# Pairs of seven products for retention's gates and second value blocks and for the last blocks of the attention's output projection, in a 256-token hybrid decoder layer on one Trainium2 core

## The chip, the cores and the metric

The kernel runs on one core of one Trainium2 chip, as one program. The core has a matrix engine (TensorE, "PE" in the profile), two engines for elementwise work that are used here (VectorE, "DVE", and ScalarE, "ACT"), GpSimd ("POOL"), and SyncE ("SP"), which mostly issues transfers. The metric is the device time of one execution in microseconds (us); lower is better. Where several executions are timed, their median is given.

## The reference

The layer takes `x` of 256 tokens by 2048 features (float32), a memory of 256 by 2048, and the weights of one decoder layer. What it computes, cut to what matters:

```python
hn = rmsnorm(x, w_mix)
z = hn @ w_in            # 2048 x 14336: q, k (1024 each), v, gate (2048 each), xr, yr, ga, gb (2048 each)
ret  = head_groupnorm(chunkwise_retention(rotary(q), rotary(k), v)) * silu(gate)   # 8 heads
rnn  = gelu(yr) * rg_lru(causal_dwconv(xr))
m    = sigmoid(ga) * (ret @ w_proj_ret) + sigmoid(gb) * (rnn @ w_proj_rnn)
h1   = x + m @ w_mix_out
h2   = h1 + cross_attention(rmsnorm(h1), rmsnorm(mem)) @ xa_w_o     # 4 heads of 512
out  = rmsnorm(h2 + (silu(gate') * val') @ ffn_w_down)              # gate', val' from a conv of rmsnorm(h2) @ ffn_w_up
```

Nearly all of the arithmetic is the product of a 256 x 2048 operand with a weight matrix. The transfers of weights total some 370 MB.

## The kernel before, in words

**Blocks and units.** Every weight matrix is cut into blocks of 512 columns (`BW`), and a block into units of 512 rows: a unit is one weight tile `raw` of 128 partitions by 4 x 512 numbers (1 MB). The list of all blocks in the order in which they are computed is written out by hand (`weight_plan`), and the transfers of the weights follow it, on SyncE's queue, into five buffers.

**Products in three parts.** Float32 accuracy is made of three products of a faster format. Each `raw` is split into `hi` (a cast on ACT, L281) and `lo = raw - hi` (on DVE, L282); each operand tile likewise. A 512-column product of 128 rows by 128 tokens is then the three products hi·hi, lo·hi and hi·lo. In `gemm_n` (token-major result) the lines are L357, L358 and L364, in `gemm_t` (feature-major result) L346. A plain block of `gemm_n` has four units of 24 products each, 96 in all.

**Pairs of seven products.** For some pairs of neighbouring blocks the kernel uses `pair_products`: half of the shared dimension of the two blocks is multiplied by a scheme of Strassen's kind with seven products instead of eight, and the other half plainly. `PAIR_UNITS` lists its eleven units in order: q1, p, q3, p, p, q5, q2, q6, p, q7, q4. The seven q's have 12 products each and the four p's ("plain") 24, 180 in all. The q's need sums of weight tiles. Two of these are made by transfers that add to what is in the buffer, issued by GpSimd (L262), and two by additions of whole tiles on DVE (L287 and L289). They also need sums of the operand's tiles, which `sums` makes (L498 to L504) and the caller passes as `ss`. The results are three accumulators, `xz`, `yu` and `rw`, and after each unit `out(kind, ...)` moves finished parts: `pair_out` into two new tiles in memory (copies L451, additions L457, subtractions L467), `pair_add` into rows that exist already (L424). There are three accumulators in all (pool `pm`), shared by pairs and plain blocks.

**What sets the order of the work around.** While one unit is multiplied, `prefetch` prepares the splits of the units after it, up to two ahead; there are three buffers each for `hi` and `lo`. Smaller work (scores and values of a retention head, its normalisation, transposes, the recurrence) is put between units by hand: `later(n, fn)` runs `fn` when n+1 further units have ended, whatever the length of these units. Within each engine, the order of instructions is fixed when the program is built, by a scheduler that works on data dependences and on the order in which the code records them; each engine then works through its own list and waits for others through semaphores.

**Retention.** Two groups g of four heads. For each, the plan has q, half of v, k, the other half of v and two blocks of gates. `retain` puts the scores of head hh after unit hh+1 that follows, the values (L515) one unit later, and after the fourth head `normalise`: statistics of DVE (L784, L785), a power on GpSimd (L607), the subtraction and gating (L797) and the scaling on ACT (L802). The transposes of heads 1 and 2 on PE (`finish_head`, L527) come two units after that, those of heads 3 and 4 three units. For the first group all this lies in the second group's q and first v block. `rotated` (L713 to L719) turns q and k on DVE.

**The operand's sums.** `x`'s scaled tiles `xs` are split once and kept. The sums of x that pairs need (`xs_sums`, four tiles) are made by `sum_x`, called inside the second and third blocks of the recurrent branch; their first reader is the pair of gates `O_GA` after it.

**Residuals.** `residual` computes mix_out and xa_w_o: blocks 0 and 1 as a pair by `pair_add`, blocks 2 and 3 plainly. After each block it takes the squares of the new rows (L1037 is such a square) and transposes them (`turn`, splits L571 and L572) into the next stage's operand, again by `later`. After xa_w_o comes ffn_up, whose k-th unit reads the transposed blocks in order. The two last stages, ffn_up and ffn_down, run in three parts; two of them use pairs for ffn_down.

The change touches `weight_plan`, `residual_plan`, the call of `out` in `pair_products`, `pair_add`, the loop over g with its gates, the place of `sum_x`, and `residual`.

Of the kernel before, what the change touches and what calls it, by code (L numbers as in the profile page):

```python
# [63 lines left out]
def weight_plan():  # L64

    w0 = "w_in"
    plan = []
    for g in range(2):
        for c in (O_Q, O_K):
            plan += [(w0, 0, NT, c + g * BW), (w0, 0, NT, O_V + g * 1024 + (c == O_K) * BW)]  # L70
        plan += [(w0, 0, NT, O_G + g * 1024 + b * BW) for b in range(2)]
    for b in range(4):
# [22 lines left out]
def residual_plan(w):  # L95
    return [(w, 0, NT, 0, BW)] + [(w, 0, NT, b * BW) for b in (2, 3)]

# [52 lines left out]
def hybrid_layer(  # L150
# [229 lines left out]
    def pair_products(w, row, st, ss, c0, c1, out):  # L380
# [18 lines left out]
        for kind, parts in units(*e):  # L399
# [18 lines left out]
            with tc.high_priority(URGENT):  # L418
                out(kind, x, z, yu, rw)

    def pair_add(w, row, st, ss, c0, c1, h0, h1):

        def add(o, i, op=ALU.add):
            dve.tensor_tensor(out=o, in0=o, in1=i, op=op)  # L424

        def out(kind, x, z, yu, rw):
            if kind == "q1":
                add(h0[:, 0, :], x)
            elif kind == "q5":
                later(2, lambda: add(h1, rw))  # L430
                later(3, lambda: add(h1, z[:, None, :].to_broadcast([P, 2, BW])))
            elif kind == "q6":
                add(h1[:, 0, :], x, ALU.subtract)
            elif kind == "q7":
                add(h0[:, 1, :], x)
                add(h1[:, 1, :], x, ALU.subtract)
            elif kind == "q4":
                add(h0, yu)

        pair_products(w, row, st, ss, c0, c1, out)  # L440
# [312 lines left out]
    def retain(g, qr, kr, vs, dec, gates):  # L753
# [51 lines left out]
        for hh in range(4):  # L805
            later(hh, lambda hh=hh: scores(hh))

    for g in range(2):
        dec = big([P, 4, S], s="dec")
        vs, turned = [], []  # L810
        for b, o in enumerate((O_Q, O_K)):
# [6 lines left out]
            if g > 0:  # L818
                turned.append(rotated(a))
            v = gemm_n("w_in", 0, xs, NT, O_V + g * 1024 + b * BW)  # L820
            if g == 0:
                turned.append(rotated(a))
            vs.append(split_rows(v, rs0))
        qr, kr = turned
        gates = []
        for b in range(2):
            a = gemm_n("w_in", 0, xs, NT, O_G + g * 1024 + b * BW)
            t = big([P, 2, BW], s="gate")
            for tt in range(2):
                act.activation(t[:, tt, :], a[:, tt, :], AF.Tanh, scale=half_rs0[:, tt : tt + 1])  # L830
            dve.scalar_tensor_tensor(out=t, in0=t, scalar=1.0, in1=a, op0=ALU.add, op1=ALU.mult)
            gates.append(t)
        retain(g, qr, kr, vs, dec, gates)
# [105 lines left out]

    xs_sums = []  # L940

    def sum_x(i):

        t = tmp("xt")
        sp.dma_start(out=t, in_=x_t[:, 2 * i : 2 * i + 2, :])
        for j in range(2):
            act.activation(t[:, j, :], t[:, j, :], AF.Identity, scale=p_mix(2 * i + j))
        xs_sums.append(sums(t))

    merged, merged_sums = [], []  # L950
# [11 lines left out]
    for b in range(4):  # L962
        if b in (1, 2):
            for i in range(2):
                later(2 + 4 * i, lambda i=2 * b - 2 + i: sum_x(i))
        recurrent(b)
# [36 lines left out]
    def residual(w, st, ssum, out, osum, wcol, steps=None):  # L1003

        ss = sp_.tile([P, 2, 4], F32, tag="ss0", name=nm("ss"))
        for bs in ((0, 1), (2,), (3,)):
            if steps:
                steps(bs[0])
            if len(bs) > 1:
                pair_add(w, 0, st, ssum, 0, BW, hrow[0], hrow[1])  # L1010
            else:
                h = hrow[bs[0]]
                dve.tensor_add(h, h, gemm_n(w, 0, st, NT, bs[0] * BW))
            for i, b in enumerate(bs):
                squares(hrow[b], ss, b)
                for pr in range(2):
                    later(2 * i + pr, lambda b=b, pr=pr: turn(b, pr, out, osum, wcol))
        return ss
# [286 lines left out]
```

## Time and profile before

| | |
|---|---|
| device time, median of 3 runs | 2017.65 us (2015.16 to 2017.88) |
| the profiled execution | 2014.64 us, of which the span of the trace is 2012.9 us |
| PE (TensorE) busy | 1999.0 us, 99% of the span, 10120 products |
| DVE (VectorE) busy | 1528.7 us, 76% |
| ACT (ScalarE) busy | 1131.6 us, 56% |
| POOL (GpSimd) busy | 36.0 us, 2% |
| transfers | 426.77 MB, 212 GB/s on average |
| granted clock of PE | 0.999 of full speed on average |

The profile is of one execution. A group line names a line of the kernel, the engine, the operation, what is written and read, and how often; then the busy time in us and the mean of one in ns, and behind the last bar the idle time of that engine just before, with what ended most of it. A line of the timeline gives the start and the duration in us, and in square brackets the idle time before it. Products on PE overlap: the next starts before the record of the last ends, so the time that one costs is read from the distance of the starts.

### The profile page before, as it was taken

The page shows a single profiled execution, that of the slowest core. Times are in us where ns is not written, and L with a number is a line of the kernel's source. Part 1 is how long each engine was busy: PE and PEld are TensorE (multiplying, and loading weights), DVE is VectorE, ACT ScalarE, POOL GpSimd, SP SyncE. Part 2 cuts the span into 40 slices and gives each one's busy share as a digit, 9 for nine tenths or more (in the row PEclk, how much of TensorE's full clock was granted, in tenths as well). Part 3 has the DMA queues.
Part 4 walks back from the last instruction along what each step waited for, and adds up shares of the span by engine and source line. Part 5 has one row for each costly group of instructions (what it writes and reads, how often), then busy time and mean ns, then how long its engine had stood idle before and what let it go on. Part 6 is the DMA issues. An engine that isn't in the chain of part 4 may idle for free.

```text
span 2012.9 us, 24896 instructions
## 1 busy us (share of the span) xinstructions
PE 1999.0 (99%) x10120; PEld 1702.0 (85%) x10120; DVE 1528.7 (76%) x1551; ACT 1131.6 (56%) x1143; POOL 36.0 (2%) x44
## 2 busy tenths in 40 slices
PE   9999999999999999999999999999999999999998
PEld 8888888888888888888888888888878888888887
DVE  6747657889985887778888767587797787886775
ACT  6445446777765554566666655455554555544552
POOL 0000000000000000000000000000000000000000
PEclk9999999999999999999999999999999999999999
DMA  9554555655887765777886746454567555675552
GB/s 369 217 205 160 209 199 184 218 195 165 246 270 260 224 235 188 229 277 221 262 270 205 249 147 230 169 198 179 187 209 232 202 186 196 187 232 187 202 196 84
DMA packets 75426, 426.77 MB, mean 212 GB/s; under 512 B 8240, under 2 KB 12976, under 8 KB 28080
## 3 DMA queue, kind: packets, MB, share of 16 engines
q1 hardware_dynamic: 69184, 389.00, 52.8%
q0 software_dynamic: 4608, 33.56, 9.0%
q10 hardware_dynamic: 1520, 2.63, 0.4%
q8 instruction: 79, 1.29, 0.2%
q14 instruction: 35, 0.29, 0.0%
HBM read 414.67 MB, written 10.49 MB: 211 GB/s over the span
## 4 chain that ended last, share of the span: by engine, by line
PE 93%; DVE 3%; DMA 1%; ACT 1%; issue 1%; SPq 0%; POOLq 0%; ACTq 0%; DVEq 0%
PE acc L346 37%; PE acc L357 17%; PE acc L364 17%; PE acc L358 17%; PE sm L515 2%; DVE lo L282 2%; DMA raw<-in_wall 1%; PE sm L527 1%; PE acc L515 1%; PE sm L874 1%; ACT hi L281 1%; DVE nat L424 0%; DVE fv L1180 0%; DVE raw L289 0%; DMA xt<-in_mem_t 0%
## 5 line engine op out<-in xcount | busy, mean ns | idle before, releaser
L282 DVE TENSOR_TENSOR lo<-raw,hi 128x2048 fp32r<-128x2048 f32 (+1 forms) x408 | 922.8, 2268 | 359.3 <-ACT hi L281 358.5
L281 ACT CAST hi<-raw 128x2048 fp32r<-128x2048 f32 (+1 forms) x406 | 771.0, 1902 | 647.6 <-PE acc L358 366.3
L357 PE MATMUL acc<-hi,s 128*128 128x512 f32 x1416 | 554.5, 392 | 0.7 <-DVE nat L424 0.7
L358 PE MATMUL acc<-hi,s 128*128 128x512 f32 x1416 | 551.7, 390 | 0.2 <-DVE s L572 0.2
L346 PE MATMUL acc<-s,hi 128*128 128x512 f32 x2176 | 518.6, 391 | 0.9 <-DVE hi L279 0.8
L346 PEld LDWEIGHTS acc<-s,hi 128*128 128x128 f32 x2176 | 402.8, 189 | 80.5 <-issue 1.3
L364 PE MATMUL acc<-lo,s 128*128 128x512 f32 x1416 | 353.8, 389 | 0.0
L357 PEld LDWEIGHTS acc<-hi,s 128*128 128x128 f32 x1416 | 265.7, 188 | 56.4 <-ACT hi L281 1.5
L364 PEld LDWEIGHTS acc<-lo,s 128*128 128x128 f32 x1416 | 265.8, 188 | 55.3
L358 PEld LDWEIGHTS acc<-hi,s 128*128 128x128 f32 x1416 | 265.9, 188 | 55.0 <-DVE s L572 0.8
L346 PEld LDWEIGHTS acc<-s,lo 128*128 128x128 f32 x2176 | 277.7, 192 | 9.6 <-DVE lo L282 0.8
L346 PE MATMUL acc<-s,lo 128*128 128x256 f32 x2176 | 282.9, 284 | 0.2 <-DVE lo L282 0.2
L357 PE MATMUL acc<-hi,ss 128*128 128x512 f32 x256 | 101.7, 397 | 2.6 <-DVE nat L424 2.6
L358 PE MATMUL acc<-hi,ss 128*128 128x512 f32 x256 | 100.0, 390 | 0.0
L537 ACT COPY c<-acc 128x512 f32<-128x512 f32 x68 | 39.1, 578 | 71.8 <-PE acc L346 71.6
L364 PE MATMUL acc<-lo,ss 128*128 128x512 f32 x256 | 68.9, 390 | 0.0
L357 PEld LDWEIGHTS acc<-hi,ss 128*128 128x128 f32 x256 | 48.1, 188 | 15.3 <-DVE nat L424 4.1
L364 PEld LDWEIGHTS acc<-lo,ss 128*128 128x128 f32 x256 | 48.0, 188 | 10.2
L358 PEld LDWEIGHTS acc<-hi,ss 128*128 128x128 f32 x256 | 48.1, 188 | 9.4
L262 POOL DMA_DIRECT2D raw<-in_wall x32 | 28.2, 883 | 1343.9 <-DVE lo L282 821.6
L538 DVE TENSOR_TENSOR uz<-acc,c 128x512 f32<-128x512 f32 x44 | 30.2, 687 | 19.9 <-ACT c L537 19.9
L424 DVE TENSOR_TENSOR nat<-nat,acc 128x512 f32<-128x512 f32 (+1 forms) x42 | 37.6, 911 | 5.6 <-PE acc L364 5.4
(233 smaller groups left out, 1217.9 us busy)
## 6 DMA issues: line engine op xcount, KB each, us to landing
raw<-in_wall SPq DMA_DIRECT2D x337, 1024.0 KB, 4.9
raw<-in_wall POOLq DMA_DIRECT2D x32, 1024.0 KB, 8.3
xt<-in_x_t SPq DMA_DIRECT2D x11, 256.0 KB, 6.4
raw<-in_wall SPq DMA_DIRECT2D x5, 512.0 KB, 8.1
nat<-in_x ACTq DMA_DIRECT2D x4, 512.0 KB, 10.6
ret<-hd SPq DMA_DIRECT2D x8, 256.0 KB, 6.1
rnn<-rn SPq DMA_DIRECT2D x8, 256.0 KB, 2.1
kt<-ret SPq DMA_DIRECT2D x8, 256.0 KB, 6.5
```

The lines of the kernel that those rows point to most:

```text
L262: pool.dma_start(out=raw, in_=src, accum_op=ALU.add)
L281: act.copy(hi[:, a:b], raw[:, a:b])
L282: dve.tensor_tensor(out=lo[:, a:b], in0=raw[:, a:b], in1=hi[:, a:b].bitcast(F32), op=ALU.subtract)
L346: pe.matmul(a, part, sx, start=k == 0 and t == 0, stop=k == nk - 1 and t == 0, skip_group_check=True)
L357: pe.matmul(o, h, hi, start=start and kk == 0, stop=False, skip_group_check=True)
L358: pe.matmul(o, l, hi, start=False, stop=False, skip_group_check=True)
L364: pe.matmul(o, h, lo, start=False, stop=stop and kk == KC - 1, skip_group_check=True)
L424: dve.tensor_tensor(out=o, in0=o, in1=i, op=op)
L515: pe.matmul(o, a, b, start=start and i == 0, stop=stop and i == 2, skip_group_check=True)
L527: pe.transpose(t[:, j, tt * P : (tt + 1) * P], rows[:, tt, k + j * P : k + (j + 1) * P], ident)
L537: act.copy(c, a[:, :, S:BW])
L538: dve.tensor_tensor(out=o, in0=a[:, :, 0:S], in1=c, op=ALU.add)
```

## The change

Four pairs of blocks that were two plain blocks each become pairs of seven products: the gates of group 0, the second value blocks (those of group 1, u), the gates of group 1, and blocks 2 and 3 of xa_w_o. In the plan the two value blocks of group 1 stand together, between q and k of that group; before, the second stood behind k. `head_gate` makes a gate in place from a pair's result. `sum_x` moves to the second value block of group 0, once per unit, its code unchanged, and its sums are kept from there on. In `pair_add`, the addition of `rw` is made at the third plain unit (`"p3"`, at the raised priority of `out`), where before it was put by `later` to two units behind q5. In `residual`, a table says which blocks are pairs; for the pair (2, 3) both transposes of block 2 come after one unit that follows, and both of block 3 after the next.

```diff
 def weight_plan():
-    for g in range(2):
-        for c in (O_Q, O_K):
-            plan += [(w0, 0, NT, c + g * BW), (w0, 0, NT, O_V + g * 1024 + (c == O_K) * BW)]
-        plan += [(w0, 0, NT, O_G + g * 1024 + b * BW) for b in range(2)]
+    v, u = O_V, O_V + 1024
+    plan += [(w0, 0, NT, O_Q), (w0, 0, NT, v), (w0, 0, NT, O_K), (w0, 0, NT, v + BW), (w0, 0, NT, O_G, O_G + BW)]
+    plan += [(w0, 0, NT, O_Q + BW), (w0, 0, NT, u, u + BW), (w0, 0, NT, O_K + BW)]
+    plan += [(w0, 0, NT, O_G + 1024, O_G + 1024 + BW)]
...
 def residual_plan(w):
-    return [(w, 0, NT, 0, BW)] + [(w, 0, NT, b * BW) for b in (2, 3)]
+    return [(w, 0, NT) + tuple(b * BW for b in bs) for bs in RESIDUAL[w]]
+
+RESIDUAL = {"w_mix_out": ((0, 1), (2,), (3,)), "xa_w_v": ((0, 1), (2,), (3,)), "xa_w_o": ((0, 1), (2, 3))}
...
             with tc.high_priority(URGENT):
-                out(kind, x, z, yu, rw)
+                out(f"p{plain}" if kind == "p" else kind, x, z, yu, rw)
...
             if kind == "q1":
                 add(h0[:, 0, :], x)
+            elif kind == "p3":
+                add(h1, rw)
             elif kind == "q5":
-                later(2, lambda: add(h1, rw))
                 later(3, lambda: add(h1, z[:, None, :].to_broadcast([P, 2, BW])))
...
+    def sum_x(i):
+        t = tmp("xt")
+        sp.dma_start(out=t, in_=x_t[:, 2 * i : 2 * i + 2, :])
+        for j in range(2):
+            act.activation(t[:, j, :], t[:, j, :], AF.Identity, scale=p_mix(2 * i + j))
+        xs_sums.append(sums(t))
+
+    def head_gate(a, t):
+        for tt in range(2):
+            act.activation(t[:, tt, :], a[:, tt, :], AF.Tanh, scale=half_rs0[:, tt : tt + 1])
+        dve.scalar_tensor_tensor(out=t, in0=t, scalar=1.0, in1=a, op0=ALU.add, op1=ALU.mult)
+        return t
...
             if g > 0:
                 turned.append(rotated(a))
-            v = gemm_n("w_in", 0, xs, NT, O_V + g * 1024 + b * BW)
-            if g == 0:
+                if b == 0:
+                    vs += [split_rows(v, rs0) for v in pair_out("w_in", xs, xs_sums, O_V + 1024)]
+            else:
+                if b == 1:
+                    for i in range(KC):
+                        later(i, lambda i=i: sum_x(i))
+                v = gemm_n("w_in", 0, xs, NT, O_V + b * BW)
                 turned.append(rotated(a))
-            vs.append(split_rows(v, rs0))
+                vs.append(split_rows(v, rs0))
         qr, kr = turned
-        gates = []
-        for b in range(2):
-            a = gemm_n("w_in", 0, xs, NT, O_G + g * 1024 + b * BW)
-            t = big([P, 2, BW], s="gate")
-            for tt in range(2):
-                act.activation(t[:, tt, :], a[:, tt, :], AF.Tanh, scale=half_rs0[:, tt : tt + 1])
-            dve.scalar_tensor_tensor(out=t, in0=t, scalar=1.0, in1=a, op0=ALU.add, op1=ALU.mult)
-            gates.append(t)
+        gates = [head_gate(a, big([P, 2, BW], s="gate")) for a in pair_out("w_in", xs, xs_sums, O_G + g * 1024)]
         retain(g, qr, kr, vs, dec, gates)
...
     for b in range(4):
-        if b in (1, 2):
-            for i in range(2):
-                later(2 + 4 * i, lambda i=2 * b - 2 + i: sum_x(i))
         recurrent(b)
...
-        for bs in ((0, 1), (2,), (3,)):
+        for bs in RESIDUAL[w]:
...
-                pair_add(w, 0, st, ssum, 0, BW, hrow[0], hrow[1])
+                pair_add(w, 0, st, ssum, bs[0] * BW, bs[1] * BW, hrow[bs[0]], hrow[bs[1]])
...
                 for pr in range(2):
-                    later(2 * i + pr, lambda b=b, pr=pr: turn(b, pr, out, osum, wcol))
+                    later(i if bs[0] and len(bs) > 1 else 2 * i + pr, lambda b=b, pr=pr: turn(b, pr, out, osum, wcol))
```

Lines behind the change move by up to ten: L527 before is L531 after, L424 is L427.

More of the change, by code (lines that the diff above doesn't have):

```diff
@@ L806, in retain @@
             later(hh, lambda hh=hh: scores(hh))
+    xs_sums = []
+    def sum_x(i):
[9 more added lines that the diff above has]
+        return t
     for g in range(2):
@@ L938, in recurrent @@
         later(0, lambda: recur(b, rgw, xr, gl))
[L940 to L948, printed above, removed]
     merged, merged_sums = [], []
```

## The prediction, made before the changed kernel was timed

> **What bounds the kernel now.** I read the page's span and engine shares first, then the chain that ended last, the waits of TensorE (PE), and a table of windows cut where the weight blocks begin (their first products located in the trace). From the page:
>
> ```profile
> span 2012.9 us, 24896 instructions
> PE 1999.0 (99%) x10120; PEld 1702.0 (85%) x10120; DVE 1528.7 (76%) x1551; ACT 1131.6 (56%) x1143; POOL 36.0 (2%) x44
> PE 93%; DVE 3%; DMA 1%; ACT 1%; issue 1%; SPq 0%; POOLq 0%; ACTq 0%; DVEq 0%
> L282 DVE TENSOR_TENSOR lo<-raw,hi 128x2048 fp32r<-128x2048 f32 (+1 forms) x408 | 922.8, 2268 | 359.3 <-ACT hi L281 358.5
> L281 ACT CAST hi<-raw 128x2048 fp32r<-128x2048 f32 (+1 forms) x406 | 771.0, 1902 | 647.6 <-PE acc L358 366.3
> ```
>
> PE is busy 99% of the span and is 93% of the chain: a product less is time saved, if PE does not wait instead. The largest work beside it is the split of the weights, 2.27 us of VectorE (DVE) and 1.90 us of ScalarE (ACT) a unit. Windows (stretch, us, then busy time and instructions of PE, PEld, DVE, ACT, POOL, granted clock, DMA share, GB/s):
>
> ```profile
> 75.07:96.86 21.79, 21.79 (x99) 18.03 (x97) 16.21 (x15) 10.13 (x8) 0.00 (x0) 1.00 0.53 189
> 96.86:140.38 43.52, 43.52 (x194) 36.04 (x192) 20.97 (x11) 19.05 (x14) 0.00 (x0) 1.00 0.54 194
> 168.60:193.21 24.61, 24.61 (x123) 20.67 (x122) 21.24 (x35) 16.39 (x25) 1.82 (x1) 1.00 0.31 109
> 564.18:604.98 40.80, 40.80 (x181) 33.78 (x180) 34.66 (x22) 27.42 (x24) 0.88 (x1) 1.00 0.78 244
> 1458.43:1542.57 84.14, 82.44 (x362) 67.21 (x361) 74.55 (x55) 46.02 (x32) 2.62 (x3) 1.00 0.69 217
> ```
>
> The second row is two plain blocks, the gates of the first four heads; the fourth is a pair of seven products that is there already. Each product of 512 columns takes 0.2267 us (43.52/192 = 40.80/180), and PE never rests in either. The pair has a wait-free example, but its DVE is at 85% (34.66 of 40.80) where two plain blocks leave it at 48%: what else DVE must do there matters.
>
> **1. Products.** A plain block has 96 products, a pair 180 for two blocks. Four pairs of blocks change: 4 x (192 − 180) = 48 products, x 0.2267 = **−10.9 us**. In the built order PE has 10,072 products for 10,120.
>
> **2. The two ffn_down pairs** use the same pair code, in which `add(h1, rw)` moves to the third plain unit.
>
> ```profile
> PE acc L357 <- DVE nat L424: 3.3, 4, 1.4
> 1495.23 1.22 DVE L424 TENSOR_TENSOR nat<-nat,acc 128x1024 f32<-128x1024 f32 x1
> 1496.37 2.28 DVE L282 TENSOR_TENSOR lo<-raw,hi 128x2048 fp32r<-128x2048 f32 x1
> 1498.57 1.22 DVE L424 TENSOR_TENSOR nat<-nat,acc 128x1024 f32<-128x1024 f32 x1
> 1499.84 0.50 PE L357 MATMUL acc<-hi,ss 128*128 128x512 f32 x1 [1.37 <-DVE nat L424]
> ```
>
> This is all that PE waits for DVE's L424: 3.3 us in four waits. The two L424 rows are the additions of `rw` and of `z`; PE cannot begin the next pair's product before the second has ended (1499.79). With the first out of the way earlier, the `z` addition runs ahead of the split L282 and ends near 1496.4, before PE asks; the short wait that follows goes too. **−3.4 us** in both pairs (rounded; ends: 0, if another split slips in between, and −4). The mix_out pair shows no such wait and gains nothing.
>
> **3. A wait that is new, in the pair of second value blocks.** Call T its start (168.60 before). In that stretch the first four heads of retention are finished: after the values of the fourth head, DVE does statistics and the rotation of Q, and only then are the heads scaled and transposed on PE.
>
> ```profile
> 168.06 2.29 DVE L282 TENSOR_TENSOR lo<-raw,hi 128x2048 fp32r<-128x2048 f32 x1 [2.65 <-ACT hi L281]
> 171.47 0.56 DVE L769 TENSOR_TENSOR ps<-pret,ps 128x384 fp32r<-128x384 f32 x1 [0.58 <-ACT ps L768]
> 171.95 0.75 DVE L784 BATCH_NORM_STATS2 bn<-rc 128x6 f32<-128x256 f32 x2
> 172.62 1.27 DVE L538 TENSOR_TENSOR q<-acc,c 128x512 f32<-128x512 f32 x2
> 181.59 0.16 DVE L605 TENSOR_SCALAR rv<-mv 128x8 f32<-128x8 f32 x1
> 183.68 0.36 DVE L793 TENSOR_SCALAR ro<-ro,ro 128x4 f32<-128x4 f32 x2 [1.54 <-POOL ro L607]
> 184.95 2.29 DVE L282 TENSOR_TENSOR lo<-raw,hi 128x2048 fp32r<-128x2048 f32 x1
> ```
>
> ```profile
> 181.83 1.82 POOL L607 TENSOR_TENSOR ro<-rv,mhalf 128x8 f32<-128x8 f32 x1 [142.35 <-DVE rv L605]
> 183.95 2.91 ACT L802 ACTIVATE rc<-rc,ro 128x256 f32<-128x256 f32 x7 [2.47 <-DVE ro L793]
> ```
>
> ```profile
> 174.07 1.24 PE L515 MATMUL sm<-v,ps 128*128 128x256 f32 x9
> 186.05 1.04 PE L527 MATMUL sm<-cid,rc 128*128 128x128 f32 x8
> ```
>
> Before, a unit is 5.44 us (96/4 products): values after the first (174.07 = T+5.47), transposes L527 after the third, at T+17.45, and the scaling L802 starts at T+15.35: it just fits. The tasks fall due by count of units, and a pair's units are shorter. Now the values come after q1 (12 products, 2.72 us) and the transposes after q3: T + 2.72 + 1.07 + 5.44 + 2.72 = T+11.95 if PE never waits, with the transposes done at T+12.74. DVE meanwhile does not get earlier. In the built order the `lo` of the second plain unit now stands ahead of the statistics; its `hi` can be cast once q1 has freed a buffer, T+2.72 + 1.9 = T+4.7, so that `lo` ends at T+6.97. Three rests of PE follow. The values wait for `ps`, ready at 172.03 = T+3.43: 0.7 us, done at T+4.5. The first plain unit needs the accumulator of Q, which is free when DVE has joined Q's halves, just behind that `lo`: T+6.97 + 0.4 (half of the `bn` row) + 0.6 (half of L538) = T+8.0, a rest of 3.5 us; it and q3 then end at T+16.2. The run from `bn` to `rv` is 9.64 us (171.95 to 181.59) and from `rv` to the first L802 2.36 us (to 183.95): T+18.97; two heads are four of these at 0.42 us (2.91/7), the first at T+19.8, a rest of 3.6 us, and the last four transposes end at T+21.2. **+8.4 us** against T+12.74, in rests of 0.7, 3.5 and 3.6 us and small ones. Behind it in PE's order stands everything else, so it is all on the path. Low end 0, if that `lo` and the rotation do not stand in the way; 3.5 if only the accumulator's wait comes. I take 8.4, which the built order gives. The same tasks for the other four heads fall into plain blocks (XR), as before.
>
> **4. The clock after such a rest.** PE rests longer than 3 us only at both ends of this trace.
>
> ```profile
> 5.64 1.19 PE L346 MATMUL acc<-s,hi 128*128 128x512 f32 x2 [0.80 <-DVE hi L279]
> 7.70 1.05 PE L346 MATMUL acc<-s,hi 128*128 128x512 f32 x2
> 8.55 0.41 PE L346 MATMUL acc<-s,lo 128*128 128x256 f32 x1
> 10.26 0.41 PE L346 MATMUL acc<-s,hi 128*128 128x512 f32 x1
> 2004.41 0.28 PE L515 MATMUL acc<-hi,s 128*128 128x256 f32 x1
> 2005.00:2010.00 5.00, 0.00 (x0) 0.00 (x0) 1.94 (x6) 1.33 (x2) 0.56 (x1) 0.71 0.44 145
> 2010.00:2012.90 2.90, 0.00 (x0) 0.00 (x0) 0.00 (x0) 0.00 (x0) 0.00 (x0) 0.50 0.29 111
> ```
>
> At the end the mean clock of 0.71 in 2005 to 2010 is 2.1 us at 1 and 2.9 at 0.5: it drops some 2.4 us after the last product (2004.69). At the start two products take 0.85 us (7.70 to 8.55), 0.427 each, until 10.26: 4.6 us at half rate from 5.64, 2.3 us lost. The rest of 3.5 us should thus halve the clock, and the 2.3 us are lost in the first plain unit and q3, which then end at T+18.5; but they only wait for the heads until T+19.8, so the loss lies inside the next rest (then 1.3 us): **0 us**. Ends: 0, and +2.3 if the clock falls in the third rest instead.
>
> [...]
>
> **5. The tail of xa_w_o.** Blocks 2 and 3 now end together: both blocks' squares and 16 transposes go into the first units of ffn_up.
>
> ```profile
> 1278.92:1299.47 20.55, 20.55 (x124) 18.11 (x122) 12.26 (x13) 9.35 (x13) 0.71 (x1) 1.00 0.49 183
> L572 DVE SCALAR_TENSOR_TENSOR s<-sm,pb,s 128x256 fp32r<-128x256 f32 x24 | 11.2, 479 | 3.3 <-ACT s L571 3.3
> ```
>
> That stretch has 8.3 us of DVE free (20.55 − 12.26); a block more adds 8 L572 = 3.8 us and the squares, but PE wants the last splits at once, and `lo`s stand ahead of some. **+1.0 us** for a wait of two L572, nearest to what this start shows now (none seen); ends 0 and 4 (all eight late).
>
> **6. Priced at nothing, with what hides it.**
>
> ```profile
> L289 DVE TENSOR_TENSOR raw<-raw,raw 128x2048 f32<-128x2048 f32 x16 | 36.6, 2290 | 0.4
> L457 DVE TENSOR_TENSOR o<-o,acc 128x1024 f32<-128x1024 f32 x16 | 19.4, 1213 | 0.0
> L500 DVE TENSOR_TENSOR sm<-xt 128x128 f32<-128x128 f32 x8 | 2.3, 287 | 2.9 <-ACT xt L947 2.9
> L504 DVE TENSOR_TENSOR ss<-sm,ss 128x512 fp32r<-128x512 f32 x24 | 16.5, 686 | 2.3 <-ACT ss L503 2.1
> raw<-in_wall POOLq DMA_DIRECT2D x32, 1024.0 KB, 8.3
> ```
>
> A pair has 11 splits for 8, two additions of raw weights (L289, L287) and the output additions (L457): about +14 us of DVE, 35 of 40.8, as in the existing pair without a wait. Of nine weight transfers two are accumulating ones issued by GpSimd (POOL), 8.3 us to landing; 8 more MB-sized issues there (32 to 40) meet a POOL that is 2% busy, and its one `pow` in the pair (row 181.83) is not behind them. SP's weight queue carries as many blocks less the two. The four `sum_x` (on DVE four additions like L500 and one L504, 1.8 us each) now lie in 75.07 to 96.86, with 5.6 us of DVE free for 7.4: some 2 us run into the gates' pair, which reads a sum first in q3, 36 products or 8.2 us after its start. If that cover is gone, PE waits up to 2 us there. SP's x_t loads of these stand ahead of weight loads that have long been issued. Where `sum_x` was (recurrent blocks) PE does not wait, so nothing is gained.
>
> **Sum:** −10.9 − 3.4 + 8.4 + 0 + 1.0 = **−4.9 us**. The profiled run took 2014.64 us (2012.9 span and 1.7 around it); the median of the runs, 2017.65, is 3.0 us above. So 2009.7 for such a run, **2012.8 us** for the median: −0.24%. I count within 0.2% (4.0 us, 2013.6 to 2021.7) as the same, about what a measurement can tell; the forecast lies at the edge.
>
> **The rivals.**
> A, the forecast, chance 0.47: rests of 7 to 10 us together, with or without a clock loss of 2.3 us; own range 2010.5 to 2016.
> B, 0.25: the rests are under 2 us together. For it: the order binds only engine by engine, and most of 171.95 to 181.59 is rotation, which shortens if its operands come early and the `lo` ahead of it does not wait. Against it: those are 9.6 us of busy DVE, not of waiting. −10.9 − 3.4 + 1.0 + 1 = −12.3: 2005.3, faster.
> [...]
> E, 0.09: the gain of step 2 does not come, as another split takes the place: −4.9 + 3.4 = −1.5, 2016.2, the same.
> F, 0.05: only the accumulator's wait, no loss of clock: −10.9 − 3.4 + 3.5 + 1 = −9.8, 2007.9, faster.
>
> **How the numbers follow.** Faster is B, F and the lower part of A (0.20 of its 0.47, as 2012.8 is just under the edge and a clock loss is over it): 0.50. Slower is C: 0.14. The same is the rest, 0.36. The range from 2004.5 (B with no rest at all is 2004.4) to 2019.5 (E with the clock loss and 1 us more of tail) leaves out C and the edges, about 0.18.
>
> **What would show it.** Step 1: a pair window of 40.80 us with 180 products at 96.86. Step 2: no wait of PE on L427 in ffn_down. Step 3: in the values' pair, a PE wait at the first plain unit (L360, released by DVE's join L542) and one with L531 behind it, released by ACT's scaling; no such waits mean B. Step 4: granted clock under 1 there, products at 0.427 us. Step 5: PE waits on L575/L576 at ffn_up's start. The prediction is wrong above all if the DVE run of 9.64 us is ordered or timed otherwise than I read it.

## The result and the profile after

The changed kernel takes 2012.28 us (median of 17 runs, 2010.55 to 2014.48), the kernel before 2015.85 us (17 runs, 2013.83 to 2017.88): a ratio of 0.9982, 95% interval 0.9975 to 0.9990. It is faster by 3.6 us (2.0 to 5.0). That is clear of no change, and just short of the 0.2% from which the prediction counts a kernel as faster; by its own count this is "the same", to which it gave 0.36, and 0.50 to "faster". The profiled execution took 2012.84 us.

The page of the changed kernel:

```profile
span 2011.0 us, 24902 instructions
PE 1992.9 (99%) x10072; PEld 1694.9 (84%) x10072; DVE 1584.5 (79%) x1588; ACT 1160.2 (58%) x1167; POOL 42.8 (2%) x52
PE 91%; DVE 4%; issue 2%; DMA 1%; ACT 1%; POOL 0%; SPq 0%; POOLq 0%; ACTq 0%; DVEq 0%
```

There are 48 products less, as counted. Less of the end's chain is PE (91% for 93%): other engines now hold it up at places. The windows of the changed kernel, cut at the changed blocks (stretch, us, busy time and instructions of PE, PEld, DVE, ACT, POOL, granted clock, DMA share, GB/s), show where:

```profile
98.45:168.59 70.14, 69.62 (x360) 59.43 (x359) 60.58 (x63) 41.27 (x38) 1.73 (x2) 1.00 0.65 216
168.59:220.37 51.78, 48.01 (x207) 38.56 (x206) 42.15 (x45) 31.27 (x38) 2.61 (x2) 0.93 0.51 161
242.59:283.48 40.89, 40.89 (x183) 33.73 (x181) 36.94 (x36) 24.42 (x20) 0.86 (x1) 1.00 0.62 202
283.48:312.82 29.34, 28.52 (x181) 25.59 (x179) 24.41 (x48) 13.70 (x14) 0.00 (x0) 1.00 0.69 243
1193.38:1460.48 267.10, 267.10 (x1445) 231.20 (x1444) 210.42 (x220) 148.74 (x153) 4.23 (x5) 1.00 0.58 196
1460.48:1542.76 82.28, 82.14 (x362) 67.39 (x361) 75.58 (x55) 46.42 (x32) 2.62 (x3) 1.00 0.70 224
```

The same stretches of the kernel before that were not shown yet:

```profile
96.86:168.60 71.74, 71.74 (x372) 61.69 (x371) 38.42 (x38) 30.55 (x25) 0.00 (x0) 1.00 0.53 192
280.84:309.06 28.22, 28.22 (x180) 25.66 (x179) 17.45 (x27) 11.50 (x12) 0.00 (x0) 1.00 0.53 188
1188.56:1458.43 269.87, 269.87 (x1457) 233.46 (x1456) 196.45 (x210) 143.90 (x150) 2.49 (x3) 1.00 0.55 191
```

Row by row: the first gates and q together are 1.6 us shorter, where 2.7 were due. The pair of second value blocks takes 51.8 us, at a mean clock of 0.93. The gates of the second group are 2.6 us shorter (43.52 before), but XR's first block behind them is 1.1 us longer (29.34 for 28.22). From xa_w_o to the end of the first ffn_up, the gain is 2.8 us. The first two ffn_down pairs are 1.9 us shorter (84.14 before), the other two 1.7.

The waits of PE in the changed kernel (in all, how often, the longest) name the largest single one:

```profile
PE acc L360 <- DVE q L542: 3.5, 1, 3.5
PE acc L361 <- DVE s L576: 1.0, 2, 0.8
PE acc L349 <- DVE o L471: 0.8, 1, 0.8
```

The four waits for the addition in `pair_add` (L424 before, L427 now) are gone. The second row is new too and stands outside the changed blocks: it lies in the pair behind mix_out (the first of xa_w_q), which took 43.42 us for 42.42 before. In the profiles of the experiments, none of which changes this place, the same pair took between 42.0 (experiment 1) and 44.0 us (experiment 7), so this differs from one profile to the next. The first row is the accumulator of q, of which the timeline of PE tells more:

```profile
171.47 1.69 PE L519 MATMUL sm<-v,ps 128*128 128x256 f32 x9
176.62 0.76 PE L360 MATMUL acc<-hi,s 128*128 128x512 f32 x1 [3.46 <-DVE q L542]
177.18 0.63 PE L361 MATMUL acc<-hi,s 128*128 128x512 f32 x1
177.61 0.63 PE L360 MATMUL acc<-hi,s 128*128 128x512 f32 x1
187.90 1.74 PE L531 MATMUL sm<-cid,rc 128*128 128x128 f32 x8
189.40 0.48 PE L360 MATMUL acc<-hi,s 128*128 128x512 f32 x1
```

DVE's timeline in the same stretch:

```profile
173.26 2.29 DVE L285 TENSOR_TENSOR lo<-raw,hi 128x2048 fp32r<-128x2048 f32 x1 [1.24 <-ACT hi L284]
175.47 0.42 DVE L788 BATCH_NORM_STATS2 bn<-rc 128x6 f32<-128x256 f32 x1
175.80 1.27 DVE L542 TENSOR_TENSOR q<-acc,c 128x512 f32<-128x512 f32 x2
185.11 0.17 DVE L609 TENSOR_SCALAR rv<-mv 128x8 f32<-128x8 f32 x1
```

With T = 168.59, the split ahead of q's join (DVE's addition of q's two halves, L542) ends at 175.55 = T+7.0, and PE goes on at 176.62 = T+8.0: both to the tenth as forecast. Then products start every 0.43 us (177.18 to 177.61), for 0.23 at the full clock (182.66 to 182.89): half rate. The window of exactly that time in the changed kernel:

```profile
175.75:182.55 6.80, 5.93 (x14) 4.70 (x15) 6.66 (x14) 1.21 (x2) 0.00 (x0) 0.50 0.43 157
```

The clock fell at 175.75, 2.6 us after the record of the last product before the rest ends (171.47 + 1.69), and stayed down until 182.55. PE is through with the transposes (L531) at 189.40 = T+20.8, where the prediction had T+21.2.

### The profile page after: what moved, and what is told of

The parts are those of the page before. It is cut to its first block, busy times and chain, and to the rows that moved or that the text cites. A ratio compares the mean times of both kernels' runs of the same rounds, so it can differ in the third digit from the quotient of the medians.

```text
span 2011.0 us, 24902 instructions
## 1 busy us (share of the span) xinstructions
PE 1992.9 (99%) x10072; PEld 1694.9 (84%) x10072; DVE 1584.5 (79%) x1588; ACT 1160.2 (58%) x1167; POOL 42.8 (2%) x52
## 4 chain that ended last, share of the span: by engine, by line
PE 91%; DVE 4%; issue 2%; DMA 1%; ACT 1%; POOL 0%; SPq 0%; POOLq 0%; ACTq 0%; DVEq 0%
PE acc L349 37%; PE acc L367 17%; PE acc L360 17%; PE acc L361 17%; DVE lo L285 2%; PE sm L519 1%; DMA raw<-in_wall 1%; PE sm L531 1%; PE acc L519 1%; ACT hi L284 1%; PE sm L893 1%; DVE fv L1186 0%; DMA xt<-in_mem_t 0%; DVE nat L427 0%; DVE raw L292 0%
## 5 line engine op out<-in xcount | busy, mean ns | idle before, releaser
L285 DVE TENSOR_TENSOR lo<-raw,hi 128x2048 fp32r<-128x2048 f32 (+1 forms) x420 | 949.7, 2267 | 315.8 <-ACT hi L284 314.4
L284 ACT CAST hi<-raw 128x2048 fp32r<-128x2048 f32 (+1 forms) x418 | 794.1, 1902 | 630.4 <-PE acc L361 329.7
L360 PE MATMUL acc<-hi,s 128*128 128x512 f32 x1336 | 524.9, 393 | 3.6 <-DVE q L542 3.5
L361 PE MATMUL acc<-hi,s 128*128 128x512 f32 x1336 | 522.1, 391 | 1.0 <-DVE s L576 1.0
L367 PE MATMUL acc<-lo,s 128*128 128x512 f32 x1336 | 335.3, 389 | 0.0
L360 PEld LDWEIGHTS acc<-hi,s 128*128 128x128 f32 x1336 | 251.8, 189 | 56.2 <-issue 3.6
L361 PEld LDWEIGHTS acc<-hi,s 128*128 128x128 f32 x1336 | 252.0, 189 | 53.3 <-DVE s L576 1.9
L367 PEld LDWEIGHTS acc<-lo,s 128*128 128x128 f32 x1336 | 250.8, 188 | 52.2
L360 PE MATMUL acc<-hi,ss 128*128 128x512 f32 x320 | 126.8, 396 | 0.6 <-ACT o L455 0.4
L361 PE MATMUL acc<-hi,ss 128*128 128x512 f32 x320 | 124.9, 390 | 0.0
L367 PE MATMUL acc<-lo,ss 128*128 128x512 f32 x320 | 86.0, 390 | 0.0
L360 PEld LDWEIGHTS acc<-hi,ss 128*128 128x128 f32 x320 | 60.1, 188 | 15.9 <-ACT o L455 1.6
L367 PEld LDWEIGHTS acc<-lo,ss 128*128 128x128 f32 x320 | 60.0, 188 | 12.7
L361 PEld LDWEIGHTS acc<-hi,ss 128*128 128x128 f32 x320 | 60.1, 188 | 11.8
L542 DVE TENSOR_TENSOR uz<-acc,c 128x512 f32<-128x512 f32 x44 | 30.2, 686 | 20.7 <-ACT c L541 20.7
L427 DVE TENSOR_TENSOR nat<-nat,acc 128x512 f32<-128x512 f32 (+1 forms) x49 | 43.9, 909 | 3.1 <-PE acc L367 3.1
```

The costliest lines, as they stand in the source:

```text
L284: act.copy(hi[:, a:b], raw[:, a:b])
L285: dve.tensor_tensor(out=lo[:, a:b], in0=raw[:, a:b], in1=hi[:, a:b].bitcast(F32), op=ALU.subtract)
L360: pe.matmul(o, h, hi, start=start and kk == 0, stop=False, skip_group_check=True)
L361: pe.matmul(o, l, hi, start=False, stop=False, skip_group_check=True)
L367: pe.matmul(o, h, lo, start=False, stop=stop and kk == KC - 1, skip_group_check=True)
L542: dve.tensor_tensor(out=o, in0=a[:, :, 0:S], in1=c, op=ALU.add)
```

## The experiments

All ratios are to the kernel before, on the same chip and in the same rounds; its median there was 2015.45 to 2015.54 us. Times are medians, and so are the differences in us; with 5 to 11 runs of a kernel the interval of a ratio spans 3.6 to 5.2 us, and ratio and difference can disagree by up to 1 us.

**1. The values plain again.**

```diff
-    plan += [(w0, 0, NT, O_Q + BW), (w0, 0, NT, u, u + BW), (w0, 0, NT, O_K + BW)]
+    plan += [(w0, 0, NT, O_Q + BW), (w0, 0, NT, u), (w0, 0, NT, O_K + BW), (w0, 0, NT, u + BW)]
...
-                if b == 0:
-                    vs += [split_rows(v, rs0) for v in pair_out("w_in", xs, xs_sums, O_V + 1024)]
+                vs.append(split_rows(gemm_n("w_in", 0, xs, NT, O_V + 1024 + b * BW), rs0))
```

> The changed kernel with its second value blocks back as two plain blocks at their old places (q, u0, k, u1); the other three pairs, the sums of x and the early addition of rw stay. Theory A (the pair of second value blocks costs PE 8.1 us of rests and half clock, from 181.3 to 189.4 in the changed profile, against 2.7 us for 12 products less): 8.1 - 2.7 = 5.4 us faster than the changed kernel, about 2006.9 us or 8.9 us under the kernel before; no rest over 1 us there, granted clock 1.00 throughout. Rival B (the pair is worth its 2.7 us, and what was lost went elsewhere, in the start, XR and xa_w_q): 2.7 us slower than the changed kernel, about 2015.0.

This kernel takes 2004.88 us, ratio 0.9947 (0.9934 to 0.9959): 10.6 us under the kernel before, 7 under the changed one. Rival B falls: this pair, as placed, costs more than it saves. The gain is larger than the 5.4 us expected, in the main because XR's first block went back to 28.2 us as well (its window in this run):

```profile
275.99:304.22 28.23, 28.23 (x181) 25.66 (x179) 20.86 (x31) 13.72 (x14) 0.00 (x0) 1.00 0.66 225
```

**2. The pair behind k.**

```diff
-    plan += [(w0, 0, NT, O_Q + BW), (w0, 0, NT, u, u + BW), (w0, 0, NT, O_K + BW)]
+    plan += [(w0, 0, NT, O_Q + BW), (w0, 0, NT, O_K + BW), (w0, 0, NT, u, u + BW)]
...
-                if b == 0:
+                if b == 1:
                     vs += [split_rows(v, rs0) for v in pair_out("w_in", xs, xs_sums, O_V + 1024)]
```

> The changed kernel with the pair of second value blocks moved one block later in the plan, behind k of its group: the heads' end then falls into k's units of 5.44 us, as it did into a plain value block before. Theory A (the cost is the place: short units with the heads' tasks and a join behind a split): the heads cost nothing; the pair's first plain unit may still wait for the join of k's halves behind the third unit's split, about 2.2 us (T+4.9 against T+2.7) and too short to halve the clock. 8.1 - 2.2 = 5.9 us faster than the changed kernel, about 2006.4; 8.1 us faster, 2004.2, if that wait does not come. Rival B (the wait is part of any such pair next to retention, or moves along with it): within 2 us of the changed kernel, 2010 to 2014.

This kernel takes 2004.92 us, 0.9952 (0.9940 to 0.9965), 10.5 us under the kernel before. The same products in the same pair, one block later, are some 7 us faster: it is the place that costs. The wait for k's join, expected at 2.2 us, was 0.6 us by the distance of the products' starts; the pair waited once more, for a subtraction (L471), and took 42.9 us for the 40.8 of its products. The expectation also called 2.2 us too short to halve the clock, as it had fallen 2.8 us into the rest in the changed kernel (so the expectation of experiment 4). A rest of 2.23 us came elsewhere in this profile, and behind it the granted clock was 0.50 (last section).

**3. The heads' transposes two units later.**

```diff
-                later(1 + hh // 2, lambda hh=hh: finish_head(g, hh, raws[hh]))
+                later(1 + hh // 2 + 2 * (g == 0), lambda hh=hh: finish_head(g, hh, raws[hh]))
```

> The changed kernel with the transposes of the first group's heads due two units later (after the third plain unit). Theory A (PE is held by the accumulator of q, 3.5 us, and by the half clock behind it, 2.9 us; the heads' scaling is only 0.7 us late by then): 0.7 us faster than the changed kernel, 2011.6, the rest before the first plain unit and the products at 0.427 us unchanged. Rival C (the heads' chain is what sets the end, and the rest only takes its place): 3 us or more faster, 2009 or less.

This kernel takes 2011.72 us, 0.9980 (0.9971 to 0.9989): 3.7 us under the kernel before, like the changed kernel. Taking the transposes away from that place gives next to nothing. The rest and the half rate stay (PE's timeline and a window of this run):

```profile
174.56 0.77 PE L360 MATMUL acc<-hi,s 128*128 128x512 f32 x1 [3.46 <-DVE q L542]
172.65:179.40 6.75, 4.84 (x12) 3.81 (x13) 6.66 (x13) 1.14 (x2) 0.00 (x0) 0.50 0.42 158
```

So the accumulator's wait with its half clock, and the heads behind it, are two holds on the same stretch: removing the second alone leaves the first. Rival C falls.

**4. The scores one unit earlier.**

```diff
-                later(1 + hh // 2, lambda hh=hh: finish_head(g, hh, raws[hh]))
+                later(1 + hh // 2 + (g == 0), lambda hh=hh: finish_head(g, hh, raws[hh]))
...
-            later(hh, lambda hh=hh: scores(hh))
+            later(max(0, hh - (g == 0)), lambda hh=hh: scores(hh))
```

> The changed kernel with the first group's scores, values and normalisation one unit earlier and the transposes left at their unit. In the built order the join of q's halves then stands behind the split of q3 and not behind that of the second plain unit. Theory A: the first plain unit waits until T+5.2 instead of T+8.0 (2.5 us, under the 2.8 us after which the clock fell), clock 1.00, no rest before the transposes: 8.1 - 2.5 = 5.6 us faster than the changed kernel, about 2006.7. Rival C (heads' chain): same sign here, but the rest before the first plain unit would be as long as before. Rival D (a rest of this length halves the clock too): products at 0.427 us for 5 to 6 us again, and only 3 us faster, 2009.5.

This kernel takes 2004.66 us, 0.9946 (0.9932 to 0.9959), 10.8 us under the kernel before. The order of the blocks is that of the changed kernel; only the heads' work starts a unit sooner, so that the statistics and q's join are no longer behind the second plain unit's split. The wait at that product and the window from q to the second gates, in this run, the changed kernel and the kernel before:

```profile
171.76 0.47 PE L360 MATMUL acc<-hi,s 128*128 128x512 f32 x1 [1.00 <-DVE mv L789]
139.47:234.57 95.10, 93.78 (x505) 80.77 (x504) 76.41 (x83) 56.53 (x61) 4.51 (x4) 1.00 0.68 213
```

```profile
141.29:242.59 101.30, 97.53 (x505) 82.97 (x504) 76.93 (x83) 56.52 (x61) 4.34 (x4) 0.97 0.63 201
```

```profile
140.38:237.32 96.94, 96.94 (x526) 84.11 (x524) 69.12 (x105) 47.39 (x54) 1.82 (x1) 1.00 0.52 187
```

6.2 us came back, and the clock stayed at 1.00 after a rest of 1.0 us. The first plain unit went on at T+3.9 (T = 167.85 here), sooner than the T+5.2 expected, so the gain is larger, too; rival C falls, and D, which asks for a rest of 2.5 us, was not put to the test here. DVE has as much to do (76.4 and 76.9 us): it was not short of time, it had its work in an order that let PE wait.

**5. The early addition alone.** The kernel before with

```diff
-                out(kind, x, z, yu, rw)
+                out(f"p{plain}" if kind == "p" else kind, x, z, yu, rw)
...
+            elif kind == "p3":
+                add(h1, rw)
             elif kind == "q5":
-                later(2, lambda: add(h1, rw))
```

> The kernel before with one edit: the addition of rw in pair_add at the third plain unit. Theory A (step 2: the four waits of PE for L424 go, and nothing comes in their place): 3.6 us faster than the kernel before (the two windows of ffn_down's pairs were 1.9 and 1.7 us shorter in the changed profile), ratio 0.9982. Rival E (another split takes the place, or the mix_out pair pays for it ahead of xa_w_q): within 1 us of the kernel before.

This kernel takes 2011.78 us, 0.9981 (0.9972 to 0.9990), 3.8 us less than the kernel before. One window of ffn_down's first pairs is 82.39 us for 84.14, and what PE still waits for L424 is

```profile
PE acc L357 <- DVE nat L424: 0.3, 1, 0.3
```

Step 2 stands, and by itself it is worth as much as the whole change.

**6. The gates plain again.** Both entries of the plan split in two, and `gemm_n` with `head_gate` in a loop in place of `pair_out`:

```diff
-        gates = [head_gate(a, big([P, 2, BW], s="gate")) for a in pair_out("w_in", xs, xs_sums, O_G + g * 1024)]
+        gates = []
+        for b in range(2):
+            a = gemm_n("w_in", 0, xs, NT, O_G + g * 1024 + b * BW)
+            gates.append(head_gate(a, big([P, 2, BW], s="gate")))
```

> The changed kernel with both gate pairs back as plain blocks; the sums of x stay where they are, as the pair of second value blocks needs them. Theory A (a pair saves 2.7 us; the first one pays 2.0 us for waits on its sums and copies, 42.8 us against 40.8; the second runs at 40.9 but holds an accumulator that XR's first block waits for, 1.1 us): 0.7 + 2.6 - 1.1 = 2.2 us slower than the changed kernel, about 2014.5. Rival B (both pairs are worth their products): 5.4 us slower, 2017.7.

This kernel takes 2015.65 us, 1.0002 (0.9994 to 1.0011): 3.4 us over the changed kernel, nearer to A (2.2) than to B (5.4), and between them. A's price for the first pair's waits was too high. The window that it came from, 42.8 us, holds 0.9 us of scores that the build had moved ahead out of q; with q, the first pair loses 1.1 us, not 2.0. With that, 1.6 + 2.6 − 1.1 = 3.1 us were due.

**7. xa_w_o's last blocks plain again.**

```diff
-RESIDUAL = {"w_mix_out": ((0, 1), (2,), (3,)), "xa_w_v": ((0, 1), (2,), (3,)), "xa_w_o": ((0, 1), (2, 3))}
+RESIDUAL = {"w_mix_out": ((0, 1), (2,), (3,)), "xa_w_v": ((0, 1), (2,), (3,)), "xa_w_o": ((0, 1), (2,), (3,))}
```

> The changed kernel with blocks 2 and 3 of xa_w_o back as plain blocks. Theory A (the tail costs nothing: xa_w_o with all of ffn_up took 267.1 us in the changed profile, 2.8 us less than before): 2.8 us slower than the changed kernel, about 2015.1. Rival (the tail costs the 1.0 us of the forecast's step 5): 1.7 us slower, 2014.0.

This kernel takes 2015.34 us, 0.9998 (0.9989 to 1.0007): 3.1 us over the changed kernel. Its window from xa_w_o to the end of the first ffn_up is that of the kernel before (269.87) to 0.02 us:

```profile
1193.12:1463.01 269.89, 269.89 (x1457) 233.54 (x1456) 196.46 (x210) 144.22 (x150) 2.50 (x3) 1.00 0.55 190
```

By these windows (267.10 with the pair) it keeps all of its 2.7 us and the tail costs nothing; the runs alone, whose interval spans 3.6 us, would not tell this from the rival's 1.7.

**8. The sums earlier, with edit 2.**

```diff
-                if b == 1:
+                if b == 0:
                     for i in range(KC):
                         later(i, lambda i=i: sum_x(i))
```

> The changed kernel with the pair of second value blocks behind k (as in the run before of that edit, 10.5 us under the kernel before) and the sums of x made in the first value block of group 0 and not in the second. Theory A (the 0.9 us that the first gate pair waits come from sums that are late): these waits go, 0.9 us faster than with the first edit alone, about 11.4 us under the kernel before, 2004.1. Rival (the waits come from the pair's own splits): no change, 2004.9; or a loss if the earlier sums hold up the first value block.

This kernel takes 2011.89 us, 0.9982 (0.9973 to 0.9991): 7 us slower than edit 2 alone. The first gates now run at their products' time, but the sums, which fell between the end of the first value block and k's end, put other work of DVE off. The first value block stayed in its accumulator until after 83.86, k held the other two, and so the next block waited for DVE's join of k (window, DVE's and PE's timeline of this run):

```profile
103.52:144.31 40.79, 40.79 (x181) 33.78 (x180) 31.67 (x17) 23.18 (x18) 0.87 (x1) 1.00 0.67 218
79.25 0.69 DVE L542 TENSOR_TENSOR q<-acc,c 128x512 f32<-128x512 f32 x1
83.86 0.74 DVE L565 SCALAR_TENSOR_TENSOR v<-acc,ro,v 128x512 fp32r<-128x512 f32 x1
80.00 0.70 PE L360 MATMUL acc<-hi,s 128*128 128x512 f32 x1 [5.07 <-DVE q L542]
```

It is the mechanism of the value pair a second time, in a plain block, and the clock fell behind this rest of 5.07 us as well: the product's record that follows, at 80.50, is 0.63 us long, as in the half rate above, for 0.39 at the full clock.

**9 to 11. The sums in k's units**, between these places, with edit 4, edit 2 and edit 1:

```diff
-                if b == 1:
-                    for i in range(KC):
-                        later(i, lambda i=i: sum_x(i))
                 v = gemm_n("w_in", 0, xs, NT, O_V + b * BW)
                 turned.append(rotated(a))
                 vs.append(split_rows(v, rs0))
+                if b == 0:
+                    for i in range(KC):
+                        later(i, lambda i=i: sum_x(i))
```

> The changed kernel with the first group's scores one unit earlier (as in the run of that edit) and the sums of x made in k's units of group 0, between the place of the changed kernel and the too early one. Theory A (the first gate pair's 2.0 us are paid for late sums, as that pair took 40.8 us where the sums were earlier; in k's units DVE has room, 18.5 of 22.2 us taken, for some of the 7.4): 2.0 us faster than with the early scores alone, 12.8 us under the kernel before, 2002.7. Rival (k's join is put off again, as it was with the sums in the first value block, where PE rested 5.2 us): 2 to 6 us slower than with the early scores alone.

> The changed kernel with the pair of second value blocks behind k of its group, and the sums of x in k's units of group 0. Theory A: 2.0 us faster than the first edit alone, 12.5 us under the kernel before, 2003.0. Rival: the join put off, 2 to 6 us slower than the first edit alone.

> The changed kernel with the second value blocks plain, and the sums of x in k's units of group 0. Theory A (the sums' place costs 2.0 us in the first gate pair, whatever follows): 2.0 us faster than the plain value blocks alone, 12.6 us under the kernel before, 2002.9; the pair of second value blocks would then show no gain of its own even where its rests are nearly gone. Rival: 2 to 6 us slower than the plain value blocks alone.

Measured, in this order: 2004.35 us, 0.9941 (0.9929 to 0.9953); 2002.77 us, 0.9939 (0.9925 to 0.9952); 2005.07 us, 0.9945 (0.9932 to 0.9957). Against the same edits with late sums that is 0.3 and 2.1 us less and 0.2 us more; the intervals overlap, so the runs do not resolve the 1.1 us of the profile. The rivals' loss did not come. The join of k is put off even further here, but the first value block has left its accumulator in time, so that the next block finds one free and PE does not wait (DVE's timeline of the second of these):

```profile
68.86 0.74 DVE L565 SCALAR_TENSOR_TENSOR v<-acc,ro,v 128x512 fp32r<-128x512 f32 x1
84.27 1.28 DVE L542 TENSOR_TENSOR q<-acc,c 128x512 f32<-128x512 f32 x2
```

In its profile the first gates with q take 69.03 us, 2.7 under the 71.74 of before, and XR's first block 28.22 as before:

```profile
96.80:165.83 69.03, 69.03 (x361) 59.44 (x359) 53.40 (x49) 38.77 (x33) 0.87 (x1) 1.00 0.66 222
273.91:302.13 28.22, 28.22 (x180) 25.66 (x179) 20.85 (x31) 13.70 (x14) 0.00 (x0) 1.00 0.65 227
```

This kernel has the lowest median of the study: 0.6% under the kernel before, faster than the changed one by more than both intervals. Whether its pair of value blocks beats plain ones stays open: 2002.8 and 2005.1 us, with ratios whose intervals overlap. In the two profiles the stretch from the first gates to XR takes 177.11 and 178.51 us, so the pair would be worth 1.4 of its 2.7 us; the runs do not resolve that.

## Why the prediction was right, and where not

The forecast was −4.9 us, measured were −3.6 (−5.0 to −2.0). The absolute time came out within 0.5 us of 2012.8, and that is luck: a sum 1.3 us too hopeful and a starting median 1.8 us above that of 17 runs offset each other.

*Step 1* (−10.9) holds: 10,072 products, and wherever nothing waits a pair takes 40.8 us.

*Step 2* (−3.4) holds: −3.6 in the two windows, −3.8 alone.

*Step 3* (+8.4) holds in size and in place. The stretch from q1 to the transposes is 8.1 us longer than without waits (189.40 against T+12.74 = 181.33). The rests fell where they were forecast: the values were through near T+4.4 (forecast T+4.5), and the second rest is 3.5 us. Counted as idle time of PE it is only 3.8 us in that window (51.78 − 48.01); the rest is products at half rate and gaps between small products, so A's "rests of 7 to 10 us together" holds only with the clock's loss counted in. Experiments 1, 2 and 4 take the mechanism away in three ways and gain some 7 us each.

*Step 4* (0 on balance) came out, with another amount. The clock fell, and the 5.9 us of products at half rate lost 3.0 us, for 2.3 forecast; so the rest at the transposes shrank to 0.7 us (eight of them take 1.74 us for 1.04 before), for 1.3. That this loss lay inside the heads' wait shows in experiment 6, where the same pair follows q and the clock fell for only half as long (3.4 us, last section). PE was through with the third unit sooner there (T+17.9 for T+19.1), and then waited 1.6 us for the heads' scaling, where the changed kernel's PE hardly waited ahead of the first transpose:

```profile
190.09 1.75 PE L531 MATMUL sm<-cid,rc 128*128 128x128 f32 x8 [1.62 <-ACT rc L806]
```

PE was through with the transposes at T+21.2 (T = 170.40 there), no earlier than the T+20.8 of the changed kernel. Experiment 3 is the reverse: the heads away, the loss stays on the path.

*Step 5* (+1.0) was wrong: 0, by the windows and by experiment 7. DVE's 8.3 free us were enough: PE is busy in all of the 267.10 us.

*Step 6* is the step that failed. "Priced at nothing" left out two waits: 1.1 us in the first gates and q, and 1.1 us at XR's first block.

The first was named there as a risk of up to 2 us, should the sums run into the gates' pair. They did, but they were in time for their reader: the last was written at 105.3 (104.57 + 0.69), and the first unit that reads one began at 106.61. What came late is other work that DVE and ACT had behind them, such as the rotation of k and an accumulator's copy (L455), for which PE waited in a later unit:

```profile
104.57 0.69 DVE L508 TENSOR_TENSOR ss<-sm,ss 128x512 fp32r<-128x512 f32 x1
116.21 0.50 PE L360 MATMUL acc<-hi,ss 128*128 128x512 f32 x1 [0.36 <-ACT o L455]
```

Where the sums were made earlier (experiments 8 to 11) the pair took 40.8 us.

The second was not seen. XR's second accumulator waits for the last subtraction of the gates' pair (L471), which stands behind a split on DVE:

```profile
282.10 0.25 DVE L865 RECIPROCAL lt<-lt 128x16 f32<-128x16 f32 x1
283.33 2.29 DVE L285 TENSOR_TENSOR lo<-raw,hi 128x2048 fp32r<-128x2048 f32 x1
285.54 0.68 DVE L471 TENSOR_TENSOR o<-o,acc 128x512 f32<-128x512 f32 x1
286.27 0.96 PE L349 MATMUL acc<-s,hi 128*128 128x512 f32 x3 [0.82 <-DVE o L471]
```

The split alone is not enough for the wait. In experiment 1, after the same pair, the subtraction stands behind a split too and PE does not wait:

```profile
274.51 2.29 DVE L285 TENSOR_TENSOR lo<-raw,hi 128x2048 fp32r<-128x2048 f32 x1 [1.33 <-ACT hi L284]
```

There the split starts 1.5 us before XR (275.99), here 0.15 us before it (283.48), because seven tiny instructions that prepare constants of the recurrence (L865 to L873, from 282.10) stand ahead of it. The build put them there in the changed kernel, in experiments 3, 4 and 7 and in the first of 9 to 11, and all of these have the wait; in the other experiments they run over 20 us earlier, and none has it. So the 1.1 us hang on DVE's order, and that changed with the place of the value pair; no run moved these instructions alone. It is again an accumulator, not DVE's share of busy time, which was the argument.

Summed with these sizes: −10.9 − 3.6 + 8.1 + 0 + 0 + 2.2 = −4.2, within the measured interval. Of the rivals, B (no rest) is nearly what experiments 2 and 4 made by hand; E's lost gain did not occur, and F falls with the loss of clock. C, which has 0.14 and lies outside the range, stands for a clock that does not come back; no run shows that: in the changed kernel it was at 0.50 until 182.55 and at 1.00 from there on (182.60 to 2000.00).

## What to carry to other kernels

When a block is replaced by one with shorter units, everything that is scheduled by counting units moves earlier on the engine that sets the time, while the work it waits for on other engines does not; ask of each such task when its inputs are ready in microseconds. Ask the same of each accumulator: the next block can begin only when the engine that empties the last one has come to it in its own order, and a 2.3 us split ahead of a 0.6 us join was enough for a rest of 3.5 us here. A pair's place in the plan was worth 7 us here, more than twice the 2.7 us that its fewer products save.

## What the runs showed of the hardware that was not expected

The stretches at half clock seen here, those at the ends of the traces aside, were 3.4 us long, or about twice that. In the changed kernel the half clock lasted 6.8 us (175.75 to 182.55), in the third experiment 6.75 us (172.65 to 179.40), and after the same rest of 3.46 us in the sixth only half of that:

```profile
178.43 0.47 PE L360 MATMUL acc<-hi,s 128*128 128x512 f32 x1 [3.46 <-DVE q L542]
178.90:182.30 3.40, 3.40 (x9) 2.63 (x9) 3.34 (x8) 0.59 (x1) 0.00 (x0) 0.50 0.73 294
```

In the second experiment a rest of 2.2 us was enough, and the clock fell only when PE was at work again. This rest lies far from the changed blocks, in xa_w_k's first pair, and comes from a copy on ACT (L457) that stood behind a wait for a transfer (`kt<-qs`):

```profile
1019.99 0.62 ACT L549 CAST s<-kt 128x512 fp32r<-128x512 f32 x1 [2.26 <-DMA kt<-qs]
1021.82 0.50 PE L360 MATMUL acc<-hi,ss 128*128 128x512 f32 x1 [2.23 <-ACT o L457]
1022.40 0.63 PE L360 MATMUL acc<-hi,ss 128*128 128x512 f32 x1
1022.40:1025.70 3.30, 3.30 (x9) 2.62 (x8) 3.30 (x4) 2.14 (x2) 0.00 (x0) 0.50 0.90 374
```

So the granted clock was 0.50 after rests of 2.2 us (experiment 2) and 3.5 us (changed kernel, experiments 3 and 6), and after the 5.1 us of experiment 8 a product's record had the length of half rate (0.63 us). After the 1.0 us of experiment 4 it stayed at 1.00 (139.47 to 234.57), and so it did after the 1.4 us of the kernel before that the prediction shows (1.00 in 1499.84 to 1510.00). For rests between 1.4 and 2.2 us no window here tells. Where the clock fell inside the rest (changed kernel, experiment 3) it stayed down for 6.8 us; where PE was already at work again (experiments 2 and 6), for 3.4 us. For experiment 2 that is an estimate from its mean clock of 0.61 in 1021.90 to 1024.00 and 0.78 in 1024.00 to 1028.00; the window above has 3.3 us of it.

So the price of a rest is not one number: beside its own length, 1.7 us (half of 3.4) or up to 3.0 us were lost, or nothing. Nor is the time until the clock falls. Counted from the end of the record of the last product before the rest, it was 1.6 us in experiment 3 (171.10 to 172.65), 2.6 us in the changed kernel and 3.9 us in experiment 6 (174.97 to 178.90), for the 2.4 us that the prediction read from the end of one trace. Its 4.6 us at the start of that trace are half rate by the distance of the products alone: the granted clock is given as 1.00 there (5.64 to 10.26), and no rest of PE in the trace ahead of it is longer than 1.1 us. Neither is a fixed delay; why these times differ, no run shows.

Such a stretch shows in the start of a run, too. In the changed kernel's profiled execution the clock fell once more in the first units, and there the longest rest of PE ahead of it in the trace is 1.1 us:

```profile
11.90:15.30 3.40, 3.40 (x12) 2.95 (x12) 2.94 (x5) 3.32 (x6) 0.00 (x0) 0.50 1.04 410
```

Its first value block begins at 32.17, that of the kernel before at 30.58, and those of experiments 1 to 4, which have the same start in their code and, by an estimate from their mean clocks (0.999, 0.998, 0.997 and 0.999, for 0.996 here), no such fall, between 29.95 and 30.36. These 1.6 us are no part of the change. Without them and without the 1.0 us behind mix_out, which differs from one profile to the next, the two spans would differ by 4.5 us and not by 1.9, near the −4.2 of the sum above; the medians, which stand for 17 executions each, differ by 3.6.
